# Values of the attention in three parts, TensorE in written order at the feed-forward net, gates of seven products

## The chip, the cores and the metric

The kernel runs on one core of a Trainium2 chip. Its engines run at the same time and wait for each other through semaphores: TensorE (PE: matrix products into the banks of PSUM; PEld is its load of stationary weights), ScalarE (ACT), VectorE (DVE), GpSimd (POOL), and SyncE (SP), which here only starts DMA transfers. The metric is device time in microseconds (us), the median over timed runs. A profile is one further execution; its span runs from the first to the last instruction, and the profiled execution's own time is a little longer than that.

## The reference

One layer of a decoder on 512 tokens of width 1024, all in float32: a windowed attention (8 heads, 2 key and value heads, width 64, window 128), beside it a gated linear attention (GLA, 4 heads), each projected and weighted with a sigmoid gate, then a SwiGLU net of width 2816, then a gated embedding, and a last norm.

```python
s = einsum('bnqhgd,bnkhd->bnhgqk', qb, kb) / 8 + bias            # blocks of 128 queries, 256 keys
pr = exp(s - m); denom = sum(pr) + exp(sink - m)
o_a = einsum('bnhgqk,bnkhd->bnqhgd', pr / denom, vb)
o_g = rms_norm(gla(q_g, k_g, v_g, log_a), gla_norm) * silu(og)
x += (sigmoid(gate_a) * (o_a @ w_proj_attn) + sigmoid(gate_g) * (o_g @ w_proj_gla)) @ w_out
g, u = split(rms_norm(x, norm_ffn) @ w_ffn_in); x += (silu(g) * u) @ w_ffn_out
x += sigmoid(rms_norm(x, norm_ple) @ w_ple_gate) * (p @ w_ple)
return rms_norm(x, norm_final)
```

## The kernel before

Nearly every product is made of three matmuls: each float32 factor is split into a high part (`fp32r`, a cast on ACT) and a low part (the difference, on DVE, now and then on POOL), and `mm3` (L122 to L124) multiplies high by high, low by high and high by low. `split` (L111, L112) does the splitting. Only a few small products take `fp32` operands as they are; one is the attention's values, L819.

A projection of 512 columns in and 512 tokens out comes in one of two forms. `fm_pair` makes it of 16 products of 512 columns (48 matmuls). `quad_pair` cuts the factors into quarters and makes it of seven products (Strassen and Winograd's scheme) of four contraction steps with 256 columns each, 84 matmuls; the sums that this needs are made of weights (DVE and POOL, L253), of the activations once, and of the results (`add`, L576 on DVE; `copy`, L580 on ACT). In a quad one bank, `pa`, is a running sum: after the first product ACT copies it out (`copy(p1, run)`), the second product on it adds to it, ACT copies again, and so on; so no later product into `pa` may start until the copy before it is done. Its order in the code is pa (b11), pb (b21), pa (t2), pc (b22), pa (t3), pb (t1), pa (t4).

Names: qk*, og*, ga*, gg* are projections for q and k, the output gate, merge gate A and merge gate G; fg* and fu* are those of the feed-forward net; gt* of the last gate. `pl*` are p @ w_ple. `sgg` is the tanh of a gate block (tanh stands for sigmoid), `sgp` that of the last gate, pov the attention's output bank, pT its transposed probabilities, pt their bank. `t2` is a rotating pool of 8 tiles of 128x512, `a8` one of 16 larger tiles.

The program writes instructions in the order of stages, and a scheduler sorts them on each engine by priorities and its own estimate, except where `manual_schedule` names engines: there they keep the written order. ACT, DVE and POOL are in written order through the feed-forward net (L1304); TensorE is sorted by the scheduler there. `issue_after(i)` puts what follows behind instruction i in the order of i's engine. `high_priority` moves an instruction up.

Transfers start on SP nearly all: weights into `raw` (L243), and with `aside` (L311) the spills to DRAM and back: `mgd` (gates), `ogd` and `ogr` (the GLA's output, written by head and read back in blocks), `pwd` (p @ w_ple). `W` hands out weights: it loads, sums (`SUMS` blocks ahead) and splits them ahead of use.

In the last stage (`ple_evac`, L1337 to L1355) each of four token tiles goes through tanh (ACT, sgp), gate and residual (DVE, L1049 and L1339), a square with sum (ACT, junk), a mean (DVE), a reciprocal root (POOL, nf0r to nf3r) and `finish`, which scales the row into `yt` on ACT (384 columns, L1326) and DVE (640 columns, L1327) and stores it. `finish(t - 1)` is called while tile t is worked on.

Of the kernel before, what the change touches and what calls it, by code (L numbers as in the profile page):

```python
# [33 lines left out]
def hybrid_layer(  # L34
# [140 lines left out]
    for i in range(4):  # L175
# [7 lines left out]
        )  # L183
    for i in range(4):
        u_rows(f"gg{i}", wk, 0, KD, C_GG + 256 * i, 256, 4)
    for i in range(4):
# [219 lines left out]
    hT = HQuads("h")  # L406
    kv = a8("kv", (P, 2, 512))
    k_aT = kv[:, 0, :]
    v_a = kv[:, 1, :].rearrange("p (t d) -> p t d", t=NT)
    v_g = [a8(f"v_g{i}", (P, NT, 512)) for i in range(2)]  # L410
# [45 lines left out]
    def v0_evac(t, ps):  # L456
        nc.scalar.copy(v_a[:, t, :], ps[:, 0:128])
        nc.vector.tensor_copy(v_g[1][:, t, 256:512], ps[:, 128:384])
        return nc.vector.tensor_copy(gk_low[:, t, :], ps[:, 384:400]).ins
# [24 lines left out]
    for _ in range(3):  # L484
        with tc.high_priority(offset=1000):
            W.split_to(len(W.ready))


# [171 lines left out]

    def stack_k():
        for g in range(2):
            split((ks[g][half[g]], kl[g][half[g]]), k_aT[half[g]], eng=nc.gpsimd)
            nc.sync.dma_start(ks[g][half[1 - g]].bitcast(F32), ks[g][half[g]].bitcast(F32))
# [11 lines left out]
    def attn_proj():  # L676
        w = W.take("ka")
        ps = bank("kaps")
        for kh in range(2):
            fm_mms(ps, (w[0][:, 4 * kh : 4 * kh + 4], w[1][:, 4 * kh : 4 * kh + 4]), ALL, hT, 4 * kh, 4, kh == 0, kh == 1)  # L680
            if kh:
                nc.scalar.copy(k_aT, ps)
                stack_k()
            yield
        yield from tok_inner("v1", hT, 0, KD, 512, lambda t, ps: nc.scalar.copy(v_g[0][:, t, :], ps))
# [64 lines left out]
    def attention():  # L750
        items = [(n, g) for n in range(NT) for g in range(2)]
        pov = {}
        pTs = {}

        v_z = t2("v_z", (P, NT, P))
        nc.gpsimd.tensor_copy(v_z, v_a)
        nc.gpsimd.memset(v_z[0:1], 0.0)

        def spans(n):
# [3 lines left out]
        def scores(j):  # L763
# [4 lines left out]
            for pair in range(2):  # L768
                ps = bank(f"sc{j}{pair}").rearrange("p (a b) -> p a b", a=2)
                keys = slice(kb * P, (n + 1) * P)  # L770
                for a in range(2):
                    h = 2 * pair + a
                    if n == 0:
                        nc.tensor.matmul(ps[:, a, :w], lhsT=qa[rows, h, tok(n)], rhs=k_aT[rows, 0:P], start=True, stop=True)
                        continue
                    q = qs[g][:, h, tok(n)]
                    nc.tensor.matmul(ps[:, a, :w], lhsT=q, rhs=ks[g][:, keys], start=True, stop=False)
                    nc.tensor.matmul(ps[:, a, :w], lhsT=q, rhs=kl[g][:, keys], start=False, stop=True)
# [14 lines left out]
            rd = sm.tile([P, 4], F32, tag="rd", name=f"rd{j}")  # L793
            nc.vector.reciprocal(rd, su)
            for a in range(4):
                nc.scalar.activation(s[:, a, :w], s[:, a, :w], AF.Copy, scale=rd[:, a : a + 1])

        def transposes(j):
# [4 lines left out]
            for b in range(nk):  # L803
                pst = bank(f"pt{j}{b}")
                for a in range(4):
                    nc.tensor.transpose(out=pst[:, tok(a)], in_=s[:, a, tok(b)], identity=ident)
                pT = t2(f"pT{j}{b}")
                with tc.high_priority(offset=300):
                    nc.scalar.copy(pT, pst)
                pTs[j].append(pT)  # L810

        def values(j):
# [3 lines left out]
            if g == 0:  # L816
                pov[n] = bank(f"pov{n}")
            for b in range(nk):
                nc.tensor.matmul(  # L819
                    pov[n][rows, :], lhsT=(v_z if b < nk - 1 else v_a)[:, kb + b, rows], rhs=pTs[j][b], start=(b == 0), stop=(b == nk - 1)  # L820
                )
# [55 lines left out]
    def gla_head(h):  # L877
# [144 lines left out]
        for j in range(2):  # L1022
# [7 lines left out]
            )  # L1030
            aside(ogd[k], o)
        yield
# [40 lines left out]
    mx = Split("mx")  # L1073

    def gates_g():
        for i in range(4):
            c = [t2(f"sgg{i}{e}") for e in range(2)]

            def evac(e, ps):
                nc.scalar.activation(c[e], ps, AF.Tanh, scale=0.5)  # L1080
                aside(mgd[i, 1, e], c[e])

            yield from fm_pair(f"gg{i}", hT, evac)

    def og_splits():
        for i in range(2):
            o = a8(f"ogr{i}")
            aside(o, ogd[4 * i : 4 * i + 4].rearrange("k p t -> p k t"))
            for h in range(2):
# [11 lines left out]
    ogs = og_splits()  # L1101
    drive(gg, ogs)
    for _ in ogs:
        pass
    for i in range(4):
# [124 lines left out]
    def p_proj():  # L1230
        for i in range(2):

            def evac(t, ps):
                o = t2(f"pl{i}{t}o")
                nc.scalar.mul(o, ps, 0.5)
                aside(pwd[t, :, 512 * i : 512 * i + 512], o)

# [30 lines left out]
    for gi, (f0, nf) in enumerate(FFN):  # L1268
# [30 lines left out]
        if gi == 0:  # L1299
            for _ in range(8):  # L1300
                next(stream)

# [27 lines left out]
    def ple_evac(i):  # L1330
        c0, ncol, _ = GATE[i]

        def evac(t, ps):
            cs = slice(c0, c0 + ncol)
            xs = xrow(t)[:, cs]
            sg = t2(f"sgp{i}{t}")[:, :ncol]
            sig = nc.scalar.activation(sg, ps[:, :ncol], AF.Tanh, scale=r3[t])  # L1337
            times_gate(sg, sg, pw[c0 // 512][:, t, c0 % 512 : c0 % 512 + ncol])
            nc.vector.tensor_tensor(out=xs, in0=xs, in1=sg, op=ALU.add)  # L1339
            ss = sm.tile([P, 1], F32, tag="ss", name=f"nf{t}{i}s")  # L1340
# [12 lines left out]
            if i == 2:  # L1353
                if t:
                    with tc.issue_after(sig.ins):  # L1355
                        finish(t - 1)
# [59 lines left out]
```

## Time and profile before

| | |
|---|---|
| timed runs | 871.78 us median of 3 (871.32 to 872.58) |
| profiled execution | 872.2 us, span 870.4 us, mean granted clock 0.998 |
| PE / PEld busy | 854.0 / 748.7 us (98% / 86%) |
| DVE / ACT / POOL busy | 565.7 / 446.2 / 160.8 us (65% / 51% / 18%) |
| DMA | 113.29 MB, mean 130 GB/s |

A row of the timeline gives the start and the length in us, the engine, the line of the kernel, the operation with what it writes and reads, and in brackets the idle time of the engine before it with what ended it. In a row with "x2" several instructions that follow each other are drawn together. An `fp32` matmul leaves two records. Lengths overlap: an engine starts its next instruction a little before the end of the last. A window's row gives each engine's busy time in that stretch and the count of instructions.

### The profile page before, as it was taken

How to read it: one execution, taken by the hardware profiler on the slowest of the kernel's cores; microseconds unless marked ns; L12 is line 12 of the kernel's file. 1: busy time of each engine (PE TensorE's matmuls, PEld its weight loads, DVE VectorE, ACT ScalarE, POOL GpSimd, SP SyncE). 2: the span in 40 equal slices, each digit the busy share in tenths (PEclk: the TensorE clock that was granted, in tenths of full speed). 3: DMA queues.
4: the chain of work that ended last, by engine and by line, in shares of the span. 5: the costliest groups of instructions: out<-in, count | busy, mean ns of one | idle time of the engine just before them, and what ended most of it. 6: DMA issues, size and time to landing. Idle time of an engine off the chain costs nothing. (4 is left out here: it accounts for less than half of the span.)

```text
span 870.4 us, 14739 instructions
## 1 busy us (share of the span) xinstructions
PE 854.0 (98%) x5901; PEld 748.7 (86%) x5901; DVE 565.7 (65%) x821; ACT 446.2 (51%) x859; POOL 160.8 (18%) x149
## 2 busy tenths in 40 slices
PE   8999989999999999999999999999999999999996
PEld 7977878888777788888887999889999889998886
DVE  5533866769876643356368799635998437985574
ACT  6336587866755543333256556413565314554453
POOL 4340434120221110100011222011232012210101
PEclk9999999999999999999999999999999999999999
DMA  9382423133764256774415233611316311422502
GB/s 282 103 215 78 152 74 97 50 102 102 236 206 158 74 170 216 271 265 146 142 54 164 94 126 108 232 49 49 95 52 211 129 49 49 136 87 94 194 1 98
DMA packets 88245, 113.29 MB, mean 130 GB/s; under 512 B 6152, under 2 KB 64304, under 8 KB 87792
## 3 DMA queue, kind: packets, MB, share of 16 engines
q1 hardware_dynamic: 86704, 107.43, 38.2%
q0 software_dynamic: 1456, 4.92, 1.6%
q8 instruction: 46, 0.75, 0.4%
q14 instruction: 23, 0.19, 0.1%
q10 hardware_dynamic: 16, 0.00, 0.0%
HBM read 95.35 MB, written 15.93 MB: 128 GB/s over the span
## 5 line engine op out<-in xcount | busy, mean ns | idle before, releaser
L111 ACT CAST fo_h<-raw 128x1024 fp32r<-128x1024 f32 x22 | 22.5, 1050 | 30.5 <-PE fo00ps L124 13.1
L112 DVE TENSOR_TENSOR fo_l<-raw,fo_h 128x1024 fp32r<-128x1024 f32 x22 | 26.3, 1220 | 12.1 <-ACT fo_h L111 12.1
L326 POOL TENSOR_TENSOR or<-om,mhalf 128x1 f32<-128x1 f32 x16 | 14.2, 886 | 68.1 <-DVE om L330 54.2
L112 DVE TENSOR_TENSOR act_l<-u,act_h 128x512 fp32r<-128x512 f32 x22 | 22.1, 1004 | 5.4 <-ACT act_h L111 5.4
L905 DVE TENSOR_TENSOR zs<-zs,kq 128x512 f32<-128x512 f32 x28 | 19.5, 707 | 7.0 <-ACT zs L901 6.3
L112 DVE TENSOR_TENSOR pg_l<-raw,pg_h 128x1024 fp32r<-128x1024 f32 x8 | 9.8, 1223 | 18.5 <-ACT pg_h L111 18.5
L112 DVE TENSOR_TENSOR wo_l<-raw,wo_h 128x1024 fp32r<-128x1024 f32 x8 | 9.8, 1224 | 17.7 <-ACT wo_h L111 17.7
L115 DVE SCALAR_TENSOR_TENSOR gt_l<-raw,gple,gt_h 128x256 fp32r<-128x256 f32 (+1 forms) x24 | 12.9, 570 | 12.0 <-ACT gt_h L114 11.9
L114 ACT ACTIVATE gt_h<-raw,gple 128x256 fp32r<-128x256 f32 (+1 forms) x24 | 12.6, 573 | 12.4 <-PE gt0ps L124 8.1
L111 ACT CAST act_h<-u 128x512 fp32r<-128x512 f32 x22 | 13.7, 622 | 10.0 <-DVE u L1283 10.0
L111 ACT CAST wo_h<-raw 128x1024 fp32r<-128x1024 f32 x8 | 8.4, 1053 | 20.1 <-PE wo0ps L124 6.6
L112 DVE TENSOR_TENSOR gg_l<-raw,gg_h 128x1024 fp32r<-128x1024 f32 x8 | 9.8, 1224 | 12.9 <-ACT gg_h L111 12.9
L899 DVE TENSOR_TENSOR zs<-G 128x512 f32<-128x512 f32 x24 | 16.1, 692 | 2.4 <-DMA G<-Gd 2.4
L111 ACT CAST pg_h<-raw 128x1024 fp32r<-128x1024 f32 x8 | 8.4, 1055 | 15.7 <-PE gg3pb L123 5.8
L112 DVE TENSOR_TENSOR v_l<-raw,v_h 128x1024 fp32r<-128x1024 f32 (+1 forms) x8 | 9.3, 1167 | 11.1 <-ACT v_h L111 11.1
L997 ACT ACTIVATE own<-o,or 128x256 f32<-128x256 f32 x16 | 7.6, 475 | 17.1 <-POOL or L326 16.9
L1283 DVE TENSOR_TENSOR u<-u,g 128x512 f32<-128x512 f32 x22 | 16.1, 733 | 0.0
L111 ACT CAST v_h<-raw 128x1024 fp32r<-128x1024 f32 (+1 forms) x10 | 9.6, 973 | 11.9 <-PE v2ps L124 4.5
L792 ACT ACTIVATE s_all<-s_all,nm 128x256 f32<-128x256 f32 (+1 forms) x32 | 15.2, 480 | 0.7 <-DVE nm L789 0.7
L112 POOL TENSOR_TENSOR qa<-qa,qs 64x768 fp32r<-64x768 f32 x2 | 7.2, 3616 | 41.6 <-ACT qs L111 41.5
L111 ACT CAST gg_h<-raw 128x1024 fp32r<-128x1024 f32 x8 | 8.4, 1049 | 12.2 <-PE ga3pb L123 4.2
L112 DVE TENSOR_TENSOR qa_l<-raw,qa_h 128x512 fp32r<-128x512 f32 x8 | 5.5, 719 | 13.2 <-ACT qa_h L111 13.2
(2312 smaller groups left out, 3550.1 us busy)
## 6 DMA issues: line engine op xcount, KB each, us to landing
raw<-in_w_ffn_in SPq DMA_DIRECT2D x44, 512.0 KB, 4.7
raw<-in_w_in SPq DMA_DIRECT2D x39, 512.0 KB, 4.7
raw<-in_w_ffn_out SPq DMA_DIRECT2D x22, 512.0 KB, 4.8
raw<-in_w_proj_gla SPq DMA_DIRECT2D x8, 512.0 KB, 5.7
mg<-mgd SPq DMA_DIRECT2D x8, 512.0 KB, 7.0
raw<-in_w_out SPq DMA_DIRECT2D x8, 512.0 KB, 4.5
raw<-in_w_ple_gate SPq DMA_DIRECT2D x8, 512.0 KB, 4.3
raw<-in_w_in SPq DMA_DIRECT2D x8, 256.0 KB, 5.0
```

The source lines that it names most:

```text
L111: ins = nc.scalar.copy(hi, src)
L112: eng.tensor_tensor(out=lo, in0=src, in1=hi.bitcast(F32), op=ALU.subtract)
L114: ins = nc.scalar.activation(hi, src, AF.Copy, scale=scale)
L115: nc.vector.scalar_tensor_tensor(out=lo, in0=src, scalar=scale, in1=hi.bitcast(F32), op0=ALU.mult, op1=ALU.subtract)
L326: return r, nc.gpsimd.tensor_tensor(out=r, in0=a, in1=mhalf, op=ALU.pow)
L792: nc.scalar.activation(s[:, a, :], s[:, a, :], AF.Exp, bias=nm[:, a : a + 1], accum_out=su[:, a : a + 1])
L899: pe.tensor_tensor(out=z3, in0=g3, in1=g3[:, :, b - 1 : b].broadcast_to([P, nb, 2 * b]), op=ALU.subtract)
L905: nc.vector.tensor_tensor(out=d4, in0=d4, in1=kq_, op=ALU.mult)
L997: nc.scalar.activation(v_[:, c, :], po[:, 0:256], AF.Copy, scale=r)
L1283: lambda: nc.vector.tensor_tensor(out=us[e], in0=us[e], in1=gs[e], op=ALU.mult),
```

## The change

Six edits. The attention's values: v is split into high and low parts (`v_s`, padded with zeros to 128 columns per group), the probabilities pT too, and each `fp32` matmul becomes three with `fp32r` operands (high by high, low v by high pT, high v by low pT). Three of the four `gg` gate blocks become quads, with ACT, DVE and POOL in written order there. TensorE is in written order for the first two blocks of the feed-forward net. The stores of `pwd` and of the gates' `mgd` start on ACT, those of `ogd` and the loads `ogr` on POOL. In the last stage `finish(t - 1)` is put behind the residual's addition on DVE instead of behind the tanh on ACT. And k's tile moves to another pool.

```diff
-    for i in range(4):
-        u_rows(f"gg{i}", wk, 0, KD, C_GG + 256 * i, 256, 4)
+    u_rows("gg0", wk, 0, KD, C_GG, 256, 4)
+    for i in range(1, 4):
+        u_quad(f"gg{i}", wk, C_GG + 256 * i)
...
+    v_s = a8("v_s", (P, 2, NT, 192), F32R)
+    v_a = v_s[:, 0], v_s[:, 1]
...
     def v0_evac(t, ps):
-        nc.scalar.copy(v_a[:, t, :], ps[:, 0:128])
+        split(
+            [v[:, t, :].rearrange("p (g d) -> p g d", d=64)[:, 0:3:2, :] for v in v_a],
+            ps[:, 0:128].rearrange("p (g d) -> p g d", g=2),
+        )
...
-                pT = t2(f"pT{j}{b}")
+                pT = [t2(f"pT{j}{b}{x}", dt=F32R) for x in "hl"]
                 with tc.high_priority(offset=300):
-                    nc.scalar.copy(pT, pst)
+                    split(pT, pst)
...
-            for b in range(nk):
+            todo = [(v, x, b) for v, x in ((0, 0), (1, 0), (0, 1)) for b in range(nk)]
+            for v, x, b in todo:
                 nc.tensor.matmul(
-                    pov[n][rows, :], lhsT=(v_z if b < nk - 1 else v_a)[:, kb + b, rows], rhs=pTs[j][b], start=(b == 0), stop=(b == nk - 1)
+                    pov[n],
+                    lhsT=v_a[v][:, kb + b, 64 * g : 64 * g + 128],
+                    rhs=pTs[j][b][x],
...
-            aside(ogd[k], o)
+            nc.gpsimd.dma_start(ogd[k], o)
...
-                aside(mgd[i, 1, e], c[e])
-            yield from fm_pair(f"gg{i}", hT, evac)
+                nc.scalar.dma_start(mgd[i, 1, e], c[e])
+            if i:
+                yield from quad_pair(f"gg{i}", hT, c, tanh, late)
+            else:
+                yield from fm_pair(f"gg{i}", hT, evac)
...
-            aside(o, ogd[4 * i : 4 * i + 4].rearrange("k p t -> p k t"))
+            nc.gpsimd.dma_start(o, ogd[4 * i : 4 * i + 4].rearrange("k p t -> p k t"))
...
-                aside(pwd[t, :, 512 * i : 512 * i + 512], o)
+                nc.scalar.dma_start(pwd[t, :, 512 * i : 512 * i + 512], o)
...
-            for _ in range(8):
-                next(stream)
+            with tc.manual_schedule(engines={nc.tensor.engine}):
+                for _ in range(8):
+                    next(stream)
...
-            sig = nc.scalar.activation(sg, ps[:, :ncol], AF.Tanh, scale=r3[t])
+            nc.scalar.activation(sg, ps[:, :ncol], AF.Tanh, scale=r3[t])
             times_gate(sg, sg, pw[c0 // 512][:, t, c0 % 512 : c0 % 512 + ncol])
-            nc.vector.tensor_tensor(out=xs, in0=xs, in1=sg, op=ALU.add)
+            added = nc.vector.tensor_tensor(out=xs, in0=xs, in1=sg, op=ALU.add)
...
-                    with tc.issue_after(sig.ins):
+                    with tc.issue_after(added.ins):
                         finish(t - 1)
```

Three places in the orders follow, each before and then after. First TensorE at the feed-forward net's first block (each row shown is the first of a product's 12 matmuls, or of the part of them that stands together). Before:

```order
L122 MATMUL fg00pa<-h_b_4366,fg00.0_h 128x256
...
L122 MATMUL fg00pb<-h_b_4367,fg00.0_h 128x256
...
L122 MATMUL fg00pc<-h_b_4368,fg00.1_h 128x256
...
L122 MATMUL fu00pa<-h_b_4366,fu00.0_h 128x256
...
L122 MATMUL fu00pb<-h_b_4367,fu00.0_h 128x256
...
L122 MATMUL fu00pc<-h_b_4368,fu00.1_h 128x256
...
L122 MATMUL fg00pa<-h_t_4370,fg00.1_h 128x256
```

After:

```order
L122 MATMUL fg00pa<-h_b_4614,fg00.0_h 128x256
...
L122 MATMUL fg00pb<-h_b_4615,fg00.0_h 128x256
...
L122 MATMUL fg00pa<-h_t_4618,fg00.1_h 128x256
...
L122 MATMUL fg00pc<-h_b_4616,fg00.1_h 128x256
...
L122 MATMUL fg00pa<-h_t_4619,fg00.2_h 128x256
```

The second product on the running bank fg00pa, which was behind fg00pc, fu00pa, fu00pb and the first two matmuls of fu00pc, now comes right behind fg00pb.

Second, ACT over the same stretch, from the split of fu00's first weights to the copies of that running bank. Before:

```order
L111 CAST fu00.0_h<-raw_4377 128x1024
L114 ACTIVATE h_t_4371<-h2t_4673 128x4x128
L111 CAST h_t_4372<-h2t_4679 128x4x128
L1235 ACTIVATE pl10o<-pl1ps_4683 128x512
L1235 ACTIVATE pl11o<-pl1ps_4684 128x512
L1235 ACTIVATE pl12o<-pl1ps_4685 128x512
L1235 ACTIVATE pl13o<-pl1ps_4686 128x512
L111 CAST fu00.1_h<-fu00.0s_4688 128x1024
L580 COPY fg00u<-fg00pa 128x256
```

After:

```order
L111 CAST fu00.0_h<-raw_4625 128x1024
L114 ACTIVATE h_t_4619<-h2t_4921 128x4x128
L1263 ACTIVATE pl10o<-pl1ps_4931 128x512
L1263 ACTIVATE pl11o<-pl1ps_4932 128x512
L111 CAST h_t_4620<-h2t_4927 128x4x128
L1264 DMA pwd<-pl10o 128x512
L1264 DMA pwd<-pl11o 128x512
L1263 ACTIVATE pl12o<-pl1ps_4933 128x512
L1263 ACTIVATE pl13o<-pl1ps_4934 128x512
L586 COPY fg00u<-fg00pa 128x256
```

The copy moved ahead of the split of fu00.1, and two DMA issues came in ahead of it; the five evacuations and splits stay ahead of it.

Third, ACT in the last stage: the last four tiles' tanh (sgp), square (junk) and scaled row (yt). Before:

```order
L1337 ACTIVATE sgp_8681<-gt2ps_8656,r_8316 128x256
L1341 ACTIVATE junk,nf02s<-xr_4211 128x256
L1337 ACTIVATE sgp_8717<-gt2ps_8692,r_8341 128x256
L1326 ACTIVATE yt<-xr_4211,nf0r 128x384
L1341 ACTIVATE junk,nf12s<-xr_4211 128x256
L1337 ACTIVATE sgp_8756<-gt2ps_8731,r_8373 128x256
L1326 ACTIVATE yt<-xr_4211,nf1r 128x384
```

After:

```order
L1367 ACTIVATE sgp_8932<-gt2ps_8907,r_8567 128x256
L1371 ACTIVATE junk,nf02s<-xr_4459 128x256
L1356 ACTIVATE yt<-xr_4459,nf0r 128x384
L1367 ACTIVATE sgp_8968<-gt2ps_8943,r_8592 128x256
L1371 ACTIVATE junk,nf12s<-xr_4459 128x256
L1356 ACTIVATE yt<-xr_4459,nf1r 128x384
L1367 ACTIVATE sgp_9007<-gt2ps_8982,r_8624 128x256
```

The row of tile t - 1 stood behind the tanh of tile t and now stands ahead of it; on DVE its other part moved the other way, from ahead of tile t's gate to behind its addition.

## Rows read from the trace of the kernel before

**Rows 1.** The page, part 1: busy time, share of the span, instructions.
```profile
PE 854.0 (98%) x5901; PEld 748.7 (86%) x5901; DVE 565.7 (65%) x821; ACT 446.2 (51%) x859; POOL 160.8 (18%) x149
```

**Rows 2.** Waits of PE: engine, line, releaser, total us, times, longest.
```profile
PE pt L806 <- ACT s_all L796: 2.4, 1, 2.4
...
PE fu00pc L122 <- ACT fu00.1_h L111: 1.1, 1, 1.1
...
PE fu00pa L124 <- DVE fu00.0_l L112: 1.0, 1, 1.0
...
PE fu00pa L122 <- ACT fu00u L580: 0.4, 1, 0.4
```

**Rows 3.** Windows: us, busy time (instructions) by engine, PEclk, DMA share, GB/s.
```profile
360.00:380.00 20.00, 20.00 (x90) 16.54 (x90) 8.79 (x10) 6.55 (x8) 3.52 (x6) 1.00 1.01 366
...
600.00:620.00 20.00, 20.00 (x169) 20.00 (x168) 15.94 (x19) 10.65 (x18) 5.68 (x4) 1.00 0.17 53
```

**Rows 4.** Timeline of PE: start, us, line, out<-in, shape, idle before.
```profile
137.08 0.28 PE L124 MATMUL qk2pc<-h_h,qk2.1_l 128*128 128x256 f32 x1
...
137.29 1.07 PE L819 MATMUL pov<-pT,v_z 128*64 128x512 f32 x2
...
139.15 0.39 PE L122 MATMUL qk2pa<-h_t,qk2.2_h 128*128 128x256 f32 x1
```

**Rows 5.** Timeline of ACT, then of DVE, in the attention.
```profile
119.33 0.35 ACT L580 COPY qk1u<-qk1pa 128x256 f32<-128x256 f32 x1
...
134.06 0.68 DVE L112 TENSOR_TENSOR qs<-pov,qs 128x512 fp32r<-128x512 f32 x1
```

**Rows 6.** Timeline of ACT at the gates gg1 and gg2.
```profile
343.98 1.04 ACT L111 CAST gg_h<-raw 128x1024 fp32r<-128x1024 f32 x1
...
344.93 0.59 ACT L1080 ACTIVATE sgg<-gg1pb 128x512 f32<-128x512 f32 x1
```

**Rows 7.** Timeline of ACT at the feed-forward net's first blocks.
```profile
470.92 1.05 ACT L111 CAST fu00.0_h<-raw 128x1024 fp32r<-128x1024 f32 x1 [1.96 <-PE fg00pb L123]
...
472.92 0.59 ACT L1235 ACTIVATE pl10o<-pl1ps 128x512 f32<-128x512 f32 x1
...
473.40 0.59 ACT L1235 ACTIVATE pl11o<-pl1ps 128x512 f32<-128x512 f32 x1
...
475.09 0.60 ACT L1235 ACTIVATE pl13o<-pl1ps 128x512 f32<-128x512 f32 x1
...
477.73 0.37 ACT L580 COPY fg00u<-fg00pa 128x256 f32<-128x256 f32 x1
```

**Rows 8.** Timeline of SP's queue: issues of pwd.
```profile
473.74 0.43 SPq L311 DMA_DIRECT2D pwd<-pl01o  x1
...
474.75 0.96 SPq L311 DMA_DIRECT2D pwd<-pl03o  x1
```

**Rows 9.** Timeline of ACT, then of DVE, in the last stage.
```profile
857.41 0.62 ACT L1326 ACTIVATE yt<-xr,nf0r 128x384 f32<-128x384 f32 x1
...
862.65 0.47 ACT L1337 ACTIVATE sgp<-gt2ps,r 128x256 f32<-128x256 f32 x1 [0.36 <-PE gt2ps L124]
...
866.17 0.61 ACT L1326 ACTIVATE yt<-xr,nf3r 128x384 f32<-128x384 f32 x1 [0.97 <-POOL nf3r L326]
...
863.26 0.55 DVE L1327 TENSOR_SCALAR yt<-xr,nf2r 128x640 f32<-128x640 f32 x1 [0.44 <-POOL nf2r L326]
...
863.73 0.42 DVE L1049 SCALAR_TENSOR_TENSOR sgp<-sgp,pw 128x256 f32<-128x256 f32 x1
```

**Rows 10.** Timeline of PE: its last matmul; then a window after it.
```profile
862.33 0.28 PE L124 MATMUL gt2ps<-gt_h,xT_l 128*128 128x256 f32 x1
...
867.20:867.40 0.20, 0.00 (x0) 0.00 (x0) 0.00 (x0) 0.00 (x0) 0.00 (x0) 0.53 0.00 0
```

**Rows 11.** Timeline of SP's queue, then of POOL, in the linear attention.
```profile
275.46 0.98 SPq L311 DMA_DIRECT2D ogd<-og  x2
...
284.48 0.55 POOL L326 TENSOR_TENSOR or<-om,mhalf 128x1 f32<-128x1 f32 x1 [13.85 <-PE lv L928]
```

More of the change, by code (lines that the diff above doesn't have):

```diff
@@ L406, in hybrid_layer @@
     hT = HQuads("h")
-    kv = a8("kv", (P, 2, 512))
-    k_aT = kv[:, 0, :]
-    v_a = kv[:, 1, :].rearrange("p (t d) -> p t d", t=NT)
+    v_s = a8("v_s", (P, 2, NT, 192), F32R)
+    v_a = v_s[:, 0], v_s[:, 1]
     v_g = [a8(f"v_g{i}", (P, NT, 512)) for i in range(2)]
@@ L486, in hybrid_layer @@
             W.split_to(len(W.ready))
+    nc.gpsimd.memset(v_s[:, :, :, 64:128].bitcast(F32), 0.0)
     bgk = cpool.tile([P, 4], F32, name="bgk")
@@ L659, in hybrid_layer, with stack_k @@
         nc.gpsimd.memset(kl[g][half[1 - g]].bitcast(F32), 0.0)
-    def stack_k():
+    ka = []
+    def stack_k(k_aT):
         for g in range(2):
@@ L678, in attn_proj @@
         ps = bank("kaps")
+        k_aT = t2("k_aT")
+        ka.append(k_aT)
         for kh in range(2):
@@ L682, in attn_proj @@
                 nc.scalar.copy(k_aT, ps)
-                stack_k()
+                stack_k(k_aT)
             yield
@@ L753, in attention @@
         pTs = {}
-        v_z = t2("v_z", (P, NT, P))
-        nc.gpsimd.tensor_copy(v_z, v_a)
-        nc.gpsimd.memset(v_z[0:1], 0.0)
         def spans(n):
@@ L773, in scores @@
                     if n == 0:
-                        nc.tensor.matmul(ps[:, a, :w], lhsT=qa[rows, h, tok(n)], rhs=k_aT[rows, 0:P], start=True, stop=True)
+                        nc.tensor.matmul(ps[:, a, :w], lhsT=qa[rows, h, tok(n)], rhs=ka[0][rows, 0:P], start=True, stop=True)
                         continue
@@ L794, in scores @@
             nc.vector.reciprocal(rd, su)
+            if nk == 2:
+                nc.vector.memset(s[:, :, 0:1], 0.0)
             for a in range(4):
-                nc.scalar.activation(s[:, a, :w], s[:, a, :w], AF.Copy, scale=rd[:, a : a + 1])
+                nc.scalar.activation(s[:, a, nk - 1 : w], s[:, a, nk - 1 : w], AF.Copy, scale=rd[:, a : a + 1])
         def transposes(j):
@@ L817, in values @@
                 pov[n] = bank(f"pov{n}")
-            for b in range(nk):
+            todo = [(v, x, b) for v, x in ((0, 0), (1, 0), (0, 1)) for b in range(nk)]
+            for v, x, b in todo:
                 nc.tensor.matmul(
-                    pov[n][rows, :], lhsT=(v_z if b < nk - 1 else v_a)[:, kb + b, rows], rhs=pTs[j][b], start=(b == 0), stop=(b == nk - 1)
+                    pov[n],
+                    lhsT=v_a[v][:, kb + b, 64 * g : 64 * g + 128],
+                    rhs=pTs[j][b][x],
+                    start=g == v == x == b == 0,
+                    stop=g == 1 and (v, x, b) == todo[-1],
                 )
@@ L1073, in hybrid_layer @@
     mx = Split("mx")
+    late, jobs = [], count()
     def gates_g():
@@ L1077, in gates_g, with evac, tanh @@
             c = [t2(f"sgg{i}{e}") for e in range(2)]
-            def evac(e, ps):
+            def evac(e, ps, c=c, i=i):
                 nc.scalar.activation(c[e], ps, AF.Tanh, scale=0.5)
-                aside(mgd[i, 1, e], c[e])
-            yield from fm_pair(f"gg{i}", hT, evac)
+                nc.scalar.dma_start(mgd[i, 1, e], c[e])
+            def tanh(e, c=c, evac=evac):
+                yield [1, next(jobs), lambda: evac(e, c[e])]
+            if i:
+                yield from quad_pair(f"gg{i}", hT, c, tanh, late)
+            else:
+                yield from fm_pair(f"gg{i}", hT, evac)
     def og_splits():
@@ L1087, in og_splits @@
             o = a8(f"ogr{i}")
-            aside(o, ogd[4 * i : 4 * i + 4].rearrange("k p t -> p k t"))
+            nc.gpsimd.dma_start(o, ogd[4 * i : 4 * i + 4].rearrange("k p t -> p k t"))
+            yield
             for h in range(2):
@@ L1101, in hybrid_layer @@
     ogs = og_splits()
-    drive(gg, ogs)
-    for _ in ogs:
-        pass
+    W.SUMS = 4
+    with tc.manual_schedule(engines={nc.scalar.engine, nc.vector.engine, nc.gpsimd.engine}):
+        for n, _ in enumerate(gg):
+            if n in (0, 3, 5, 6, 9, 11):
+                next(ogs)
+        flush(late, True)
+    W.SUMS = 5
     for i in range(4):
```

## The prediction, made before the changed kernel ran

> **What bounds the kernel now.** I read the page's busy times first: TensorE is busy 854.0 us of the span's 870.4 [rows 1], so a gain must take work from it or close one of its few pauses, and a loss is a new pause. Then the waits of TensorE [rows 2]: the longest, 2.4 us, is before the attention's first transposes and stays; at the feed-forward net's first blocks lie 1.1, 1.0 and 0.4, together 2.5 us. Then windows of pure product work, for the price of a matmul [rows 3]: 90 matmuls of 512 columns in 20 us are 0.222 us each, 169 of 256 columns are 0.118 each. The second window has the weight load busy all 20.00 us, so narrow matmuls wait for their weights, and halving the columns does not halve the time. Last, the timelines around the four places that change.
>
> **Values of the attention.** Between the last product matmul before a pair of values (137.08, after which 0.12 us is its own) and the next product (139.15) two fp32 matmuls take 1.95 us [rows 4]; six such pairs and two single ones, at 1.1 each, make 13.9 us. After: 14 x 3 = 42 matmuls of 512 columns at 0.222 = 9.3. TensorE's work falls by 4.6 us. Against it come 14 subtractions on DVE for the low parts of pT, at 0.68 each by the subtraction out of a bank [rows 5], 9.5 us, which TensorE's other products must cover. I walked the eight items with ACT's and DVE's new orders. In six the low part is there before its matmul is due, since four matmuls with high parts go first (0.9 us). In the first, the gain is lost: the next product waits for ACT's copy at 119.33, which is over at 119.68 [rows 5], where TensorE went on at 119.74 before; that takes back 0.5. In the fifth, the cast of pT41 stands behind the cast og0.3_h and behind a copy that waits for TensorE itself; I estimate 0.7 from a cast's 0.6 and a copy's 0.37 [rows 7]. Net -3.4. Ends: -4.6 if nothing is late, and +0.8 if all eight items wait for one subtraction (8 x 0.68 = 5.4); I take the value of the walk, nearer the first end.
>
> **Three gate blocks of seven products.** 48 x 0.222 = 10.66 us each becomes 84 x 0.118 = 9.94 [rows 3]: -0.73, three times -2.2. By columns alone (21,504 for 24,576) it would be -1.3 each, but the weight load does not allow that. The new form makes TensorE wait for ACT's copy of the running bank. Between the end of gg1 and that copy in gg2, ACT's order holds a copy (0.37), a tanh (0.59), the issue of its store (0.5, below), two casts of 1.04 and the copy itself [rows 6, 7]: 3.9 us, where TensorE has two products of 12 x 0.119 = 2.86 to do. That is a new wait of 1.0. At gg1 and gg3 the same sum is 1.5 and 2.9, so they go through. Net -1.2; ends -2.2 (no wait) and 0 (issues of 0.96, og_h0's transfer late).
>
> **TensorE in written order at the feed-forward net.** Before, behind fg00pb TensorE did fg00pc, fu00pa, fu00pb and two matmuls more, which gave ACT time until its copy of fg00pa at 477.73 [rows 7]; it paid the 2.5 us of waits. Now the second product on fg00pa comes right behind fg00pb, and it needs that copy. fg00pb ends about 470.9, when ACT starts the cast fu00.0_h, which had waited for it [rows 7]; this cast still stands ahead of the copy, and so do two casts of h_t, four evacuations pl10o to pl13o, and two issues of pwd. Starts of ACT lie 0.48 apart for such a tile (472.92 to 473.40), the large cast takes 0.95 to the next start. An issue is not in ACT's rows; on SP it took 0.43 to 0.96 [rows 8], six of eight under 0.66, so I take 0.5, and part of the first runs beside the cast in front of it. Sum: 0.95 + 6 x 0.48 + 2 x 0.5 - 0.3 + 0.37 = 4.9: the copy is over at 475.8 and TensorE stands for about 5.0 us instead of 2.5. The other six stores cost ACT 3 us, but those ahead of 470.92 fall into its idle time (1.96 us before that cast alone), and behind the copy I find every part in time. Net +2.5. Ends: issues for nothing +1.7, at 0.96 each +3.5. What is queued behind the waiting product is the rest of fg00 and all of fu00, so the stall passes on undiminished.
>
> **Last stage.** Before, ACT took the tanh of tile t first and then the row of tile t - 1. Now the row stands ahead, and it waits for POOL's root, the end of tile t - 1's chain; so the four tiles no longer overlap. From a tile's tanh to its row it is 862.65 to 866.17, 3.52 us, of which 0.55 went to DVE's part of the row in front of the gate (863.26, the gate at 863.73, where the tanh was over at 862.65 + 0.47 = 863.12) [rows 9]; without that 2.97. Then 0.5 for the row before the next tanh may start: 3.5 us a tile, above the 2.88 that TensorE gives it (24 matmuls at 0.12). The first row starts at 857.41 as before; three rounds later, at 857.41 + 3 x 3.48 = 867.85, the last one does, instead of 866.17: +1.7. TensorE ends when it did. Ends: -0.5 (the tanh is not held, and DVE's gate comes sooner) and +1.9.
>
> **The rest.** Transfers on ACT and POOL instead of SP: no wait of TensorE ended with one of these, so the emptier SP queue is worth nothing, and what they cost on ACT is counted above. On POOL the reading of ogr0 now stands before the root of head 2 at 284.48; the stores that it waits for were issued by 276.4, 8 us earlier, and POOL was idle for 13.85 us there [rows 11], so it is hidden as long as landing and issue together stay under 8 us. The split of v adds four small subtractions to DVE before the attention, beside TensorE's products: 0, at worst +0.3.
>
> Sum: -3.4 - 1.2 + 2.5 + 1.7 = -0.4. The profiled execution took 872.2 us, its span and 1.8 around it, 0.4 above the median of 871.78. From it I get 871.8, and by the same difference a median of **871.4 us**. About 1.7 us (0.2%) is what a measurement can tell from no change.
>
> **Rivals.**
> - *The work saved arrives whole* (30%). The walks on ACT are too slow and no new wait appears in the attention or at the gates: -4.6 - 2.2, with issues for nothing +1.7, last stage +1.7, together -3.4: 868.4. For it: TensorE waited almost nowhere before, and ACT is half idle. Against it: the written order of ACT at the gates is tight by the sum above.
> - *The clock falls in the 5 us pause* (20%). At the end of the program TensorE's last matmul was over at about 862.6, and by 867.2 to 867.4 the granted clock was down at 0.53, on its way to half, 1.2 GHz [rows 10]: 4.7 us of standing still was enough there. The pause forecast at the feed-forward net is as long; 2.4 us [rows 2] left the clock alone. No row shows products at the low clock, so the price lies between 0 and half the length of the low stretch; with a stretch as long as the pause, 5 us, it is 2.5: 873.9, slower. It decides if the pause comes out as long as that standing still did. The Trainium skill, TensorE: Matmul & The Clock Gate (HAM oscillation — how this bites in real kernels), says that a pause long enough puts the clock back to half and that the next burst starts cold; the trace agrees on the fall after the last matmul, and no run here shows the cold start. By that rule the time is this rival's.
> - *POOL's transfers come late* (10%). If issue and landing take over those 8 us, the root of head 2 is late and with it the output's scaling; the price is what is over, 1 to 2 us: 872.9.
> - The forecast itself has 40%. That the seven products are not faster at all is inside it: the gates' end of 0 gives 872.6.
>
> **How the numbers follow.** The forecast with its own ends covers 869.9 to 873.2 and is mostly within 0.2% of 871.78 (870.0 to 873.5); the first rival is faster, the second slower, the third on the border. Faster: 0.28 of the first, 0.04 of the forecast, 0.32. Slower: 0.18 of the second, 0.05 of the third, 0.06 of the forecast, 0.29. Same: the other 0.39. The range goes from the first rival, a little below it, to the second with a stretch half as long again: 868.0 to 875.0.
>
> **What would show it.** Values: 42 records of 0.22 us spacing, and pauses of TensorE of 0.5 us at most before them. Gates: three blocks of about 10 us, with a wait near 1 us in gg2 ended by ACT's copy. Feed-forward net: one wait of 4.3 to 6 us on the product into fg00pa, ended by the copy fg00u, in place of the three of before, and the clock still 1.00 behind it. Last stage: about 5.3 us instead of 3.6 from TensorE's last matmul to the last row on ACT, with tanh starts 3.5 us apart. If the wait at fg00pa is under 3 us, or the last tanh follows TensorE at once, the step concerned is wrong; if the clock falls, the second rival holds.

## The result, and the profile after

The changed kernel takes 877.19 us (median; 873.98 to 879.53), 1.0061 times the kernel before (95% interval 1.005 to 1.0072): slower by 5.4 us, where 871.4 was forecast and 875.0 was the upper end of the range. The profiled execution took 877.76 us, its span 876.0, with a mean granted clock of 0.988 (before 0.998).

The page's busy time, part 1, shows nothing of this: TensorE is busy as long as before [rows 1], the span is 5.6 us longer.

```profile
PE 853.7 (97%) x6023; PEld 762.3 (87%) x6023; DVE 596.0 (68%) x866; ACT 454.3 (52%) x877; POOL 172.1 (20%) x164
```

TensorE's waits (engine, line, releaser, total us, times, longest) show where it stands now:

```profile
PE fg00pa L122 <- ACT fg00u L586: 4.3, 1, 4.3
PE o L1003 <- ACT sc L1018: 3.3, 1, 3.3
PE pt L814 <- ACT s_all L804: 1.8, 1, 1.8
...
PE gg2pa L122 <- ACT gg2u L586: 0.2, 1, 0.2
```

The first takes the place of the three at the feed-forward net [rows 2], as forecast. The second is in the linear attention, where the prediction had no term. To see how much each stage gained or lost, follow the first matmul of some banks through TensorE's timeline. Before:

```profile
274.85 0.58 PE L122 MATMUL ga2pb<-h_h,ga_h 128*128 128x512 f32 x1
...
297.00 0.50 PE L122 MATMUL ga3pa<-h_h,ga_h 128*128 128x512 f32 x1
...
365.48 0.39 PE L122 MATMUL pg0pa<-og_h,pg_h 128*128 128x512 f32 x1
...
467.97 0.28 PE L122 MATMUL fg00pa<-h_b,fg00.0_h 128*128 128x256 f32 x1
...
493.96 0.28 PE L122 MATMUL fg01pb<-h_b,fg01.0_h 128*128 128x256 f32 x1
```

After:

```profile
271.95 0.58 PE L122 MATMUL ga2pb<-h_h,ga_h 128*128 128x512 f32 x1
...
299.48 0.50 PE L122 MATMUL ga3pa<-h_h,ga_h 128*128 128x512 f32 x1
...
366.83 0.40 PE L122 MATMUL pg0pa<-og_h,pg_h 128*128 128x512 f32 x1
...
469.35 0.28 PE L122 MATMUL fg00pa<-h_b,fg00.0_h 128*128 128x256 f32 x1
...
498.14 0.28 PE L122 MATMUL fg01pb<-h_b,fg01.0_h 128*128 128x256 f32 x1
```

After minus before: -2.9 at ga2pb, when the attention is done; +2.5 at ga3pa; +1.4 at pg0pa, when the gates are done; +1.4 at fg00pa; +4.2 at fg01pb. The last matmul, at 866.51, is also 4.2 later than before [rows 10], and the span 5.6. So the stages up to the end of the attention gave 2.9, the linear attention took 5.4, the gates gave 1.1, the feed-forward net's first blocks took 2.8, and the last stage 1.4.

**The linear attention.** Timelines of POOL, DVE, ACT and PE after, one row of each (start, length, engine, line, operation, in brackets the idle time before and what ended it):

```profile
273.17 1.21 POOL L1045 DMA_DIRECT2D ogd<-og  x2 [5.01 <-DVE og L1042]
...
279.89 0.69 DVE L961 TENSOR_TENSOR qd<-kq,eg 128x512 f32<-128x512 f32 x1 [4.27 <-DMA ogd<-og]
...
280.82 1.22 ACT L1018 COPY sc<-dsc 32x128 f32<-32x128 f32 x4 [4.31 <-DVE dsc L928]
...
282.09 1.22 PE L1003 MATMUL o<-own,sc 128*128 128x256 f32 x2 [3.27 <-ACT sc L1018]
```

The same DVE and PE steps before:

```profile
280.12 0.69 DVE L947 TENSOR_TENSOR qd<-kq,eg 128x512 f32<-128x512 f32 x1 [1.95 <-DMA ogd<-og]
...
282.33 0.70 PE L989 MATMUL o<-own,sc 128*128 128x256 f32 x2 [0.61 <-ACT sc L1004]
```

`qd` takes a tile of the rotating pool `t2` which an `og` held, and that `og` is the source of a store to `ogd`. DVE may write only when the store has landed. Before, DVE was idle 1.95 us for it, and TensorE had other products until all but 0.61 of the delay was over. After, everything else comes some 2.5 us earlier (DVE was free at 279.89 - 4.27 = 275.62 instead of 278.17), but the landing has hardly moved: the store is issued 2.3 us earlier than before [rows 11] and releases `qd` 0.2 earlier. From issue to release it takes 6.7 us on POOL, 4.7 before on SP. TensorE waits 2.7 us longer, and the gain of the attention is gone.

**The clock.** Windows of after (us, busy time and instructions of PE, PEld, DVE, ACT, POOL, then granted clock, DMA share, GB/s):

```profile
282.00:288.00 6.00, 5.91 (x49) 4.45 (x50) 5.64 (x11) 4.54 (x13) 1.10 (x2) 0.50 0.56 176
...
476.80:481.80 5.00, 5.00 (x24) 5.00 (x25) 0.80 (x2) 0.37 (x1) 0.00 (x0) 0.50 0.95 304
484.00:489.00 5.00, 5.00 (x44) 5.00 (x43) 3.48 (x5) 4.03 (x7) 1.29 (x1) 1.00 0.00 0
```

After both pauses TensorE runs at the lower level, 1.2 GHz, for some 6 us of products. At the feed-forward net it does 24 matmuls in 5 us there and 44 at the full clock: 5 x (1 - 24/44) = 2.3 us lost in those 5. Over the whole stretch, 476.68 to 482.80, it is 2.8: the 28 matmuls there take 6.12 us, and at 0.118 each they would take 3.30. In the linear attention the same products follow each other without a wait from the `o` that waited to the next one. That next `o`, before and then after:

```profile
287.24 0.59 PE L989 MATMUL o<-own,sc 128*128 128x256 f32 x2
```

```profile
289.73 0.60 PE L1003 MATMUL o<-own,sc 128*128 128x256 f32 x2
```

Before, this is 287.24 - 282.33 = 4.91 us; after, 289.73 - 282.09 = 7.64. So of the 5.4 lost there 2.7 were waited, and 2.7 went to the low clock. The busy time hides the low clock, since a slow matmul is busy longer.

**Feed-forward net.** ACT, its queue and PE after:

```profile
472.31 1.05 ACT L111 CAST fu00.0_h<-raw 128x1024 fp32r<-128x1024 f32 x1 [1.12 <-PE fg00pb L123]
...
475.77 0.59 ACT L1263 ACTIVATE pl13o<-pl1ps 128x512 f32<-128x512 f32 x1
475.91 0.33 ACTq L1264 DMA_DIRECT2D pwd<-pl12o  x1
476.25 0.38 ACT L586 COPY fg00u<-fg00pa 128x256 f32<-128x256 f32 x1
...
476.68 0.58 PE L122 MATMUL fg00pa<-h_t,fg00.1_h 128*128 128x256 f32 x1 [4.30 <-ACT fg00u L586]
```

From the cast to the copy's start ACT takes 3.94 us; the forecast's sum has 4.9 - 0.37 = 4.5. The large cast takes 0.95 and the six tiles behind it 0.47 to 0.54 each, with an issue between two of them or without: an issue lasts 0.33 us but runs beside the instruction ahead of it. So the two issues, 2 x 0.5 - 0.3 = 0.7 in the sum, cost almost nothing here, and TensorE's wait is 4.3 instead of 5.0.

**Last stage.** ACT after (the first row, the last two tanh and the last row):

```profile
861.23 0.62 ACT L1356 ACTIVATE yt<-xr,nf0r 128x384 f32<-128x384 f32 x1 [1.04 <-POOL nf0r L327]
...
865.22 0.46 ACT L1367 ACTIVATE sgp<-gt2ps,r 128x256 f32<-128x256 f32 x1
...
868.69 0.45 ACT L1367 ACTIVATE sgp<-gt2ps,r 128x256 f32<-128x256 f32 x1
...
871.64 0.62 ACT L1356 ACTIVATE yt<-xr,nf3r 128x384 f32<-128x384 f32 x1 [0.97 <-POOL nf3r L327]
```

The tanh starts lie 3.47 us apart (forecast 3.48), and the last row starts 5.13 after the last matmul at 866.51, where it was 3.84 [rows 9, 10].

**Values and gates.** TensorE's first transposes in the attention (`pt`), before; then after, with the first of the six matmuls of a pair of values and the next product:

```profile
114.07 1.21 PE L806 MATMUL pt<-ident,s_all 128*128 128x128 f32 x4 [2.42 <-ACT s_all L796]
```

```profile
113.57 1.35 PE L814 MATMUL pt<-ident,s_all 128*128 128x128 f32 x4 [1.85 <-ACT s_all L804]
...
136.56 0.40 PE L829 MATMUL pov<-pT20h,v_s 128*128 128x512 f32 x1
...
137.95 0.28 PE L122 MATMUL qk2pa<-h_t,qk2.2_h 128*128 128x256 f32 x1
```

The wait at `pt`, which stands ahead of the values, is 0.6 us shorter after. The six matmuls, 0.23 apart, take 1.39 us, where two took 1.95 [rows 4]. The gates' new wait in gg2 is 0.2 instead of the 1.0 walked, another of 0.5 came in gg3, and the stage gained the 1.1 that was forecast (1.2).

### The profile page after: what moved, and what is told of

It is laid out like the page before. It is cut to its first block, busy times and chain, and to the rows that moved or that the text cites. A ratio compares the mean times of both kernels' runs of the same rounds, so it can differ in the third digit from the quotient of the medians.

```text
span 876.0 us, 15080 instructions
## 1 busy us (share of the span) xinstructions
PE 853.7 (97%) x6023; PEld 762.3 (87%) x6023; DVE 596.0 (68%) x866; ACT 454.3 (52%) x877; POOL 172.1 (20%) x164
## 3 DMA queue, kind: packets, MB, share of 16 engines
q0 software_dynamic: 2640, 9.11, 3.1%
## 4 chain that ended last, share of the span: by engine, by line
PE 85%; DVE 4%; ACT 3%; issue 3%; DMA 2%; POOL 2%; SPq 1%; POOLq 0%; ACTq 0%; DVEq 0%
DMA raw<-in_w_in 1%; PE v1ps L122 1%; PE pov L829 1%; PE gt0ps L124 1%; PE v1ps L123 1%; PE gt0ps L123 1%; PE wo0ps L122 1%; PE v1ps L124 1%; PE wo1ps L122 1%; PE fo10ps L122 1%; PE fo00ps L122 1%; PE wo1ps L124 1%; PE fo10ps L123 1%; PE fo00ps L123 1%; PE wo0ps L124 1%
## 5 line engine op out<-in xcount | busy, mean ns | idle before, releaser
L914 ACT ACTIVATE zs<-zs 128x256 f32<-128x256 f32 x28 | 11.8, 421 | 6.2 <-DVE zs L913 4.1
L111 ACT CAST mx_h<-yg 128x512 fp32r<-128x512 f32 x8 | 5.0, 622 | 18.0 <-DVE yg L1141 18.0
L1305 ACT ACTIVATE g<-g 128x512 f32<-128x512 f32 x22 | 14.0, 635 | 0.0
```

Of the source, the lines that this page charges most:

```text
L111: ins = nc.scalar.copy(hi, src)
L1305: yield [1, next(jobs), lambda: nc.scalar.activation(gs[e], gs[e], AF.Silu)]
```

## The experiments

Three theories stood at first. A: the store's landing holds `qd`, and with it TensorE (5.4 us). B: the written order of TensorE costs the pause and the clock (2.8). C: the last stage (1.3). The rival to A was that DVE's added subtractions make the attention's successors late.

**gla_sp**, the store and the loads `ogr` on SP again:

```diff
-            nc.gpsimd.dma_start(ogd[k], o)
+            aside(ogd[k], o)
...
-            nc.gpsimd.dma_start(o, ogd[4 * i : 4 * i + 4].rearrange("k p t -> p k t"))
+            aside(o, ogd[4 * i : 4 * i + 4].rearrange("k p t -> p k t"))
```

> The changed kernel, but the stores of ogd and the loads ogr start on SP again. Theory: in the changed kernel the stores of head 1 land late on POOL's queue; one of their source tiles is the slot of the t2 pool that qd of the next head takes, so DVE, ACT's copy of sc and TensorE's product o wait (3.3 us at 282), and the clock falls in that pause and costs as much again. With the stores on SP the wait is under 1 us, the clock stays 1.00 from 270 to 300, and the first matmul of ga3pa comes 2 to 3 us ahead of that of the kernel before: 877.2 - 5.4 = about 871.8. Rival: the 5.4 us come from TensorE being early there (it meets some other wait): then o still waits 2 us or more and the time stays above 874.

Measured 880.18 us, 1.0099 [1.0085, 1.0113]. The time is a miss, the place is not: TensorE's wait at `o` is 0.8, the clock is 1.00 from 270 to 300, and ga3pa is 1.9 us ahead of the kernel before (2 to 3 were expected). The loss comes later. SP's queue, then ACT:

```profile
350.01 8.74 SPq L244 DMA_DIRECT2D raw<-in_w_proj_gla  x3
358.85 0.44 SPq L312 DMA_DIRECT2D ogr<-ogd  x1
...
365.31 1.04 ACT L111 CAST og_h<-ogr 128x1024 fp32r<-128x1024 f32 x1 [6.94 <-DMA ogr<-ogd]
```

The second load `ogr` stands on SP behind weight loads that hold the queue for 8.74 us. ACT stands idle for it and casts the projection's weights (`pg_h`) behind it, and TensorE waits for those:

```profile
PE pg0pa L122 <- ACT pg_h L111: 5.3, 1, 5.3
```

In the kernel before the same load was issued on SP at 342.32, and TensorE did not wait; the change also sets at which step of the gates each load is issued, which the diff above leaves out. So one of the moved transfers is worth something: the loads belong on POOL's queue, given the changed order of SP. The experiment changed two things; store_sp below, which leaves the loads on POOL, takes them apart.

**og_inplace**: `og` is written where its input lay, so that no store holds a tile of `t2`.

```diff
-            o = t2(f"og{k}")
+            o = sl[:, j, :]
```

> The changed kernel, stores still on POOL's queue, but og is written in place into its own head's tile and not into a slot of t2. Theory of the late slot: qd waits for no store any more, o's wait goes, about 871.8 as with the stores on SP. Rival, POOL's order (ogr0's issue holds up the roots of head 2, or issuing on POOL is slow as such): nothing changes, 877, since the stores stand where they stood.

Measured 871.82, 0.9998 [0.9989, 1.0007]; from 877.19 this is 5.4 us. DVE's step has no wait any more, and none at `o` is left:

```profile
275.50 0.68 DVE L961 TENSOR_TENSOR qd<-kq,eg 128x512 f32<-128x512 f32 x1
```

DVE has all its added subtractions here, so the rival to A falls.

**pe_sched**: TensorE sorted by the scheduler at the feed-forward net again.

```diff
-            with tc.manual_schedule(engines={nc.tensor.engine}):
-                for _ in range(8):
-                    next(stream)
+            for _ in range(8):
+                next(stream)
```

> The changed kernel, but TensorE is sorted by the scheduler again in the first blocks of the feed-forward net. Theory: the written order costs 2.8 us there, a pause of 4.3 us for three of together 2.5, and products at half clock behind it; it goes: about 874.4, clock 1.00 from 460 to 500. Rival: the written order is worth as much as its pause costs, because the products run without a break behind it, and the time stays at 877.

Measured 874.82, 1.0038 [1.0025, 1.0052], 2.4 under the changed kernel. The two intervals overlap a little; the same edit gives 1.5 between c_order and c_sched below, where all six runs lie under the other's lowest. The clock was not 1.00 from 460 to 500: it fell here too, behind a wait of 1.9 us.

**tail_sig**: the finish of tile t - 1 behind tile t's tanh, as before.

```diff
-            nc.scalar.activation(sg, ps[:, :ncol], AF.Tanh, scale=r3[t])
+            sig = nc.scalar.activation(sg, ps[:, :ncol], AF.Tanh, scale=r3[t])
...
-                    with tc.issue_after(added.ins):
+                    with tc.issue_after(sig.ins):
```

> The changed kernel, but finish(t - 1) stands behind the tanh again, as before. Theory: the last stage's tanh starts lie 2.9 us apart again instead of 3.47, and 1.3 us go: 875.9, with 3.8 us instead of 5.1 from TensorE's last matmul to the last row. Rival: the last stage is bound by its stores, and nothing changes.

Measured 875.56, 1.0043 [1.003, 1.0056], 1.6 under. These intervals overlap too; the same edit gives 2.0 between og_inplace and c_order below. The last tanh now starts 0.31 us after the last matmul's start, where it was 2.18.

The next two ask whether it is POOL's queue that moves the landing. **store_sp** has the stores alone on SP (the first pair of lines of gla_sp). **b_store_pool** is the kernel before, with its stores alone on POOL.

> The changed kernel with only the eight stores of ogd back on SP; the two loads ogr stay on POOL. Theory: the stores' landing on POOL's queue is what held qd's slot, and the loads of ogr on SP are what held the first weights of pg0 back when both were on SP: so here both waits are gone (o under 1 us, pg0pa none) and the time is about 872. Rival: the wait at pg0 came from the stores on SP: then it stays at 5 us and the time at 878 to 880.

> The kernel before with only the stores of ogd moved to POOL. Theory: they land later there, qd's wait grows from 1.95 us to 4 and more, o waits 2 to 3 us instead of 0.6, and the clock may fall behind it: 873.5 to 876.5. Rival: only TensorE's lead of 2.9 us over the rest of the chain made the wait; without the lead nothing changes: 871.8.

store_sp: 871.42, 0.9998 [0.9989, 1.0007], with a wait at `o` of 1.4 (under 1 was expected) and none at pg0pa. It differs from gla_sp by the two loads alone: 871.42 for 880.18. SP's queue and DVE:

```profile
272.76 0.98 SPq L312 DMA_DIRECT2D ogd<-og  x2
...
278.34 0.69 DVE L961 TENSOR_TENSOR qd<-kq,eg 128x512 f32<-128x512 f32 x1 [2.87 <-DMA ogd<-og]
```

b_store_pool: 875.82, 1.0044 [1.003, 1.0057], with a wait at `o` of 3.3. POOL and DVE:

```profile
275.19 1.20 POOL L1031 DMA_DIRECT2D ogd<-og  x2 [4.92 <-DVE og L1028]
...
282.17 0.69 DVE L947 TENSOR_TENSOR qd<-kq,eg 128x512 f32<-128x512 f32 x1 [4.54 <-DMA ogd<-og]
```

One line that moves eight stores to POOL costs the kernel before 4.2 us (875.82 against 871.64 beside it). TensorE has no lead here, so the rival (only the lead made the wait) falls; the lead has a small part of its own, since in store_sp's profile 0.8 us of it is lost at `o` with the stores on SP. From issue to release: 7.0 us on POOL and 4.7 on SP in the kernel before, 6.7 and 5.6 in the changed one.

**b_values**: the kernel before with the values in three parts alone (its lines of the diff above).

> The kernel before with only the values of the attention in three parts (and k's tile in the other pool). Theory: 3 us of lead at og3, as in the changed kernel, and nothing gives it back later: 868.8. Rival: the lead is lost at the linear attention, which waits for transfers that did not get faster: 870.5 to 871.8.

Measured 868.70, 0.9964 [0.9952, 0.9977], 2.9 faster. SP's queue and DVE:

```profile
271.87 0.98 SPq L311 DMA_DIRECT2D ogd<-og  x2
...
276.34 0.69 DVE L960 TENSOR_TENSOR qd<-kq,eg 128x512 f32<-128x512 f32 x1 [1.76 <-DMA ogd<-og]
```

With the store on SP the release comes 3.8 us earlier, in step with all else, and TensorE keeps the gain: ga3pa is 3.5 earlier than before. So the values were worth keeping; in the changed kernel the queue took what they gave.

The rest takes the two repairs together and looks at the feed-forward net. **c_order** is og_inplace with tail_sig. **c_sched** is c_order with the edit of pe_sched. **c_fill** is c_order with 36 matmuls in TensorE's pause whose results nobody reads:

```diff
+        if name == "fg00":
+            hi, _ = act.q("b21")
+            for k in range(36):
+                nc.tensor.matmul(pc[:, H[1]], lhsT=w[0][:, 1, k % 4, :], rhs=hi[:, k % 4, :], start=True, stop=True)
```

**c_act** is c_order with ACT too in written order over the two blocks (`manual_schedule(engines={nc.tensor.engine, nc.scalar.engine})`). The written order of ACT, DVE and POOL through the feed-forward net begins only behind these two blocks: in them ACT is sorted by the scheduler, in the kernel before as in the changed one.

> The changed kernel with og written in place and the last stage's order of before; TensorE still in written order at the feed-forward net's first blocks. The two repairs should add, since they lie 500 us apart: 871.8 (og in place) - 1.5 (last stage) = 870.3. Rival: the clock falls elsewhere when the phases move, and it stays near 872.

> As c_order, but TensorE sorted by the scheduler in the first blocks. If the written order costs what undoing it alone gave (2.4 us), 868; if a good part of that was the low clock, which falls by chance, 869.5. TensorE's first matmul of fg01's pb product should come about 1 to 2.5 us earlier, set against that of fg00pa, than in c_order.

> As c_order, with 36 matmuls of 256 columns that nobody reads put on TensorE between fg00pb and the second product on fg00pa: they fill the pause of 4.3 us (36 x 0.118 = 4.25). Theory: the pause costs 4.3 and the low clock behind it some 1 to 2.6 more, so the copy still comes as late, but the clock stays 1.00 from 460 to 500 and 1 to 2.6 us go: 868 to 869.3. Rival: the low clock costs nothing, since the products behind the pause wait for weights and casts anyway: no change from c_order.

> As c_order, with ACT in written order as well in the first blocks; by its order the casts fu00.0_h and fg00.3_h no longer stand ahead of the copy of fg00pa. Theory: the pause of TensorE is what stands ahead of that copy; without 1.5 us of casts and without the wait for fg00pb it falls from 4.3 to about 2.3, and the clock mostly stays up: 867 to 868.5. Rival: the casts that come later now make their products wait, and nothing is won.

c_order 869.85, 0.9978 [0.9968, 0.9988]; c_sched 868.33, 0.9955 [0.9939, 0.9971]; c_fill 868.31, 0.9964 [0.9951, 0.9977]; c_act 869.11, 0.9966 [0.9956, 0.9976]. In c_sched's profile the first matmul of fg01pb comes 2.3 us earlier after that of fg00pa than in c_order's, as expected. In the code c_order and c_fill differ by unread work alone. For each there follow a window around the pause, the first matmul behind the pause and the first of fg01pb, c_order first:

```profile
470.00:480.00 10.00, 9.50 (x66) 9.50 (x67) 5.61 (x8) 4.29 (x7) 0.00 (x0) 0.83 0.56 177
...
470.50 0.39 PE L122 MATMUL fg00pa<-h_t,fg00.1_h 128*128 128x256 f32 x1 [4.30 <-ACT fg00u L586]
...
490.82 0.28 PE L122 MATMUL fg01pb<-h_b,fg01.0_h 128*128 128x256 f32 x1
```

```profile
470.00:480.00 10.00, 10.00 (x86) 10.00 (x85) 6.32 (x8) 5.94 (x9) 0.20 (x1) 1.00 0.54 171
...
471.35 0.28 PE L122 MATMUL fg00pa<-h_t,fg00.1_h 128*128 128x256 f32 x1
...
490.06 0.28 PE L122 MATMUL fg01pb<-h_b,fg01.0_h 128*128 128x256 f32 x1
```

Adding 36 matmuls makes the kernel 1.5 us faster by the medians; the two intervals overlap, and six of c_fill's ten runs lie under the lowest of c_order's twelve. The profiles show why: the clock stays at 1.00, and of the 86 matmuls in the 10 us 13 are unread ones, which leaves 73 for 66. The product behind the pause even starts 0.85 us later, since the unread ones are not over when the copy is; from there to fg01pb TensorE takes 18.71 us instead of 20.32. ACT's order moved as well (the scheduler put the cast fu00.0_h behind the copy), but the copy starts at 469.93 for 470.07, so this is not the gain. c_act is a miss (867 to 868.5 was expected): the wait fell to 3.0 only, where 2.3 was expected, and the clock still fell behind it:

```profile
PE fg00pa L122 <- ACT fg00u L586: 3.0, 1, 3.0
```

**c_act_fill** is c_act with 26 unread matmuls in the pause.

> og in place, last stage as before, TensorE and ACT in written order in the feed-forward net's first blocks, and 26 matmuls that nobody reads (3.1 us) in the pause of 3.0 us. Theory: the low clock behind that pause costs 1 to 2 us in c_act, which keeps it out of c_act's 869.1: 867 to 868, under c_sched's 868.3 or level with it, and the clock 1.00 from 460 to 500. Rival: the pause alone decides and c_act's time stays.

Measured 867.38, 0.9947 [0.9933, 0.9961], the lowest median of all; 1.7 under c_act, with four of its five runs under the lowest of c_act's twelve. PE, then the window:

```profile
466.52 3.28 PE L600 MATMUL fg00pc<-h_b,fg00.0_h 128*128 128x256 f32 x26
```

```profile
460.00:470.00 10.00, 10.00 (x69) 9.24 (x68) 9.21 (x14) 6.92 (x13) 3.40 (x2) 1.00 0.31 115
```

TensorE does not stand still there at all, and the clock is 1.00. By the intervals it can't be told from c_sched, which needs no unread work; in its profile the scheduler's pause of 1.9 us left the clock at 1.00.

## Why the prediction was wrong

**The step that failed** is in "The rest": "no wait of TensorE ended with one of these, so the emptier SP queue is worth nothing", and "it is hidden as long as landing and issue together stay under 8 us". The first asks only whether TensorE itself waited for one of these transfers, the second only who waits for the load; neither asks who waits for the store. The store holds its source tile, and the next user of that tile was DVE. The row at 280.12 of the kernel before said so: 1.95 us of DVE's idle time ended by ogd<-og. The list of TensorE's waits names only the last link, ACT's `sc`, with 0.6, and the prediction went no further back. b_store_pool shows that the queue alone makes most of the loss (4.2 us), og_inplace that it goes when the store no longer holds the tile (5.4). That the landing moves with the queue could be weighed too: the Trainium skill, DMA: Bandwidth & Descriptors (SWDGE vs HWDGE vs iDMA), says that transfers started on GpSimd have their descriptors built by software on its cores, those of SP and ACT in hardware, and set up faster. The Trainium skill, DMA: Bandwidth & Descriptors (Specifications), gives about 1 and 0.6 us to the first byte. The rows agree in the sign and show more: from issue to release the two queues differ by 1.1 and by 2.3 us. Why it is more stays open. In the sum this was a term put at 0 that measured +5.4, half of it waiting and half the low clock behind the wait: from -0.4 it makes +5.0, which is most of the miss.

**The first rival** fell: of the 4.6 us of the values 2.4 arrived in the profile, of the 2.2 of the gates 1.1, and the last stage cost about what was forecast.

**The third rival** saw POOL's transfers late, but at the root of head 2, with 1 to 2 us. TensorE's waits have nothing there. The loads on POOL were right, as gla_sp against store_sp shows.

**The second rival held as a mechanism.** The clock did fall in the pause at the feed-forward net, though the pause was 4.3 and not 5 us, and also in one that nobody had forecast, at `o`, of 3.3. The prediction tied a fall to a pause as long as the 4.7 us of standing still that it had a row for; the clock fell behind 3.0 us in c_act too. The Trainium skill, TensorE: Matmul & The Clock Gate (HAM oscillation — how this bites in real kernels), says that the work behind a long enough pause starts cold; the windows at 282 and 476.8 show this, at 0.50. The forecast left it at 20% for want of a row of products at the low clock. Its price is 2.8 and 2.7 us in the profile of after, where the low stretches are long, and by the medians 1.5 (c_fill against c_order) and 1.7 (c_act_fill against c_act); the prediction took 2.5.

**The feed-forward net** was forecast at +2.5 and came to +2.8, from three parts of which only one was in the sum. The wait grew by 1.8 (4.3 for 2.5) and not by 2.5, since the two issues cost ACT nothing that shows. The clock took 2.8. And the kernel before lost more than its waits there: 180 matmuls at 0.118 are 21.2 of its 26.0 us from fg00pa to fg01pb, so 4.8 is lost and only 2.5 of it waited; the rest lies in steps of 0.1 to 0.3 us where one product follows another. After, the same 180 leave 7.6 of 28.8: 4.3 waited, 2.8 for the clock, 0.5 for the rest. So the written order gave back 1.8, which the sum did not have either. That the size was near is chance.

**Values:** -3.4 forecast; b_values has -2.9 by the medians. The profile of after has -2.9 at ga2pb as well, but 0.5 of that stands ahead of the values, in the shorter wait at `pt`, and is not theirs: in b_store_pool, whose attention is that of the kernel before, this wait is 1.8 too. From `pt` on the gain is 2.4. It is 2.4 in c_order's profile also, where the clock stayed at 1.00 behind that wait; after, it fell to 0.50 there (115 to 117). The matmuls cost 0.23 each instead of 0.222, together 0.4 more; which wait took the rest was not followed.

**Gates:** -1.2 forecast, -1.1 measured. The walk on ACT put the wait into the right block and gave it 1.0, of which 0.2 came, with 0.5 in gg3. No experiment changed the gates alone.

**Last stage:** +1.7 forecast, +1.4 by the spans and 1.6 by tail_sig. The pitch of 3.48 was right to 0.01. The start was off: the first row comes 5.28 us ahead of the last matmul's start, where 4.92 was assumed, as before [rows 9, 10].

## What to carry to other kernels

When a transfer goes to another queue, ask who waits for its landing through the tile that it reads: look on every engine, not on TensorE alone, for idle time that ended with that transfer, since a small wait of TensorE may be the rest of a long one elsewhere. A gain ahead of a release that does not move with it is lost there. Price a pause of TensorE like those here, of 3 to 4 us, as its length and a stretch of products at half speed behind it; if the pause has to stay, unread matmuls that fill it may make the kernel faster.

## What the runs showed of the hardware that was not expected

The store of `og` that `qd` waits for releases its tile 6.7 to 7.0 us after its issue on POOL's queue and 4.5 to 5.6 on SP's; why they differ by more than the issue itself (0.57 us on POOL, 0.32 on SP) was not settled. The page of the profile counts the transfers of POOL on a queue of their own kind, and its bytes follow the edits: 4.92 MB before, 7.01 in b_store_pool, 9.11 after.

An issue on ACT's own queue lasts 0.33 to 0.38 us and runs beside the instruction ahead of it, so it did not move the starts of the tiles at the feed-forward net. Where the store reads what the instruction just ahead writes, at the gates, ACT stood idle 0.40 us for it.

The clock does not fall by the length of the pause alone. All pauses of 3.0 to 4.3 us, at the feed-forward net and at `o`, were followed by a fall; behind the 1.9 that the scheduler leaves at the feed-forward net it fell in pe_sched and not in c_sched. Behind the wait of 1.8 us at `pt` it fell in the profiles of after, pe_sched, b_values, c_act and c_fill, and not in those of gla_sp, og_inplace, store_sp, b_store_pool, c_order, c_sched and c_act_fill; behind 2.4 us, before and in tail_sig, it did not fall. The low stretch behind the same pause of 4.3 us also differed: some 7 us in the profiles of after, store_sp and tail_sig, 3 to 4 in those of gla_sp, og_inplace and c_order. What decides this was not tried. It fits that the seven runs of the changed kernel lie 5.5 us apart, the three slowest with the lowest mean granted clock (0.988) and the fastest with the highest (0.993). The seven runs of the kernel before beside them lie 1.3 apart; in later groups they lie 2.0, 2.2 and, with one run of 27 far out, 5.5 apart.
